# Priority for the closing LayerNorms of a two-layer trunk, and a last column half made in two ranges

## The chip, the cores and the metric

The kernel runs on one core of one Trainium2 chip. The metric is the device time of one launch in microseconds. The kernel before takes 645.32 us, the median of three runs (645.12 to 645.33).

## The reference

A post-norm decoder trunk of two layers on x of 256 tokens by 1024 columns. A conditioning vector c gives six vectors per layer (shift, scale and gate, twice). Each layer is an attention and an MLP, both modulated before and closed with a LayerNorm after. With one block of 256 tokens, the block-sparse attention of layer 0 selects nothing and is plain causal attention.

```python
mod = jnp.einsum('bd,lde->lbe', jax.nn.silu(c), ada_w) + ada_b[:, None, :]
for i in range(DEPTH):                                   # 2 layers
    shift1, scale1, gate1, shift2, scale2, gate2 = [m[:, None, :] for m in jnp.split(mod[i], 6, axis=-1)]
    h = x * (1.0 + scale1) + shift1
    y = moba_attention(h, ...) if i % 2 == 0 else diff_attention(h, ...)
    x = layer_norm(DEEPNORM_ALPHA * x + (1.0 + gate1) * y, ln_g[i, 0], ln_b[i, 0])
    h = x * (1.0 + scale2) + shift2
    y = jnp.square(jax.nn.relu(h @ w_up[i])) @ w_down[i]   # 1024 -> 4096 -> 1024
    x = layer_norm(DEEPNORM_ALPHA * x + (1.0 + gate2) * y, ln_g[i, 1], ln_b[i, 1])
return x
```

## The kernel before

The 256 tokens are two blocks, b = 0 and b = 1, of 128 rows each. All weights stream from HBM once. Every dense product is exact to float32 by three matmuls (`mm3`, L164 to L166, and `dense2`, L181): the operand and the weight are each split into a rounded part and a rest, and hi by hi, hi by lo and lo by hi are added in PSUM. So each weight piece of 128x1024 costs a cast on ScalarE (ACT, L127) and a subtraction on VectorE (DVE, L128), and the activations cost the same.

The order of the work is written by hand in `PROGRAM` as short steps: V and Q make values, queries and keys; S, P, F are attention; O is the output projection; U is the MLP's product upward for one block and 512 of the 4096 columns (24 matmuls), X and Y its squared ReLU and the upward products of both blocks together; D is the product downward; B makes the vectors that a close needs; C closes a sub-layer for one block; E is the end of the last D, for b = 1, by column halves. f takes steps from a queue `filler`: each step is a DMA of 512 KB (L212) and a reduction on DVE (L213) towards the conditioning vectors. Around the first close the program reads `... O01 C00 O10 O11 C10 U00 U01 X00 ...` (for C, the first digit is b and the second says attention or MLP).

A scheduler sets each engine's own order from this: it takes instructions as their inputs become ready in its model, and in a `with tc.high_priority()` block those traced inside go ahead of others that wait. The order is then fixed; every engine runs its own list and waits on semaphores.

A close (`close`, L585) is for one block:

- `layer_norm`: z = accumulator * gate for both halves (DVE, L286), z += alpha * x (L289), statistics (L299, L300), the reciprocal square root on GpSimd (POOL, L274 and L275), the first half normalised on DVE (L305), a bias on DVE (L307), the second half normalised on ACT (L308).
- `modulate`: for each half four transposes on TensorE (PE, L317) into PSUM tile `tp`, scale and shift on ACT (L321), the rounded part hT on ACT (L324) and its rest on DVE (L325). hT is the operand of the next dense products: L164 and L165 use its rounded part, L166 its rest.
- the residual for the next close (L328, L329), which goes to the front of `filler`.

There are eight closes: for each of the two layers, after the attention and after the MLP, b = 0 and then b = 1. The text calls the pairs close 1 (layer 0 attention, at 135 to 159 us), close 2 (layer 0 MLP, 318 to 345), close 3 (layer 1 attention, 440 to 465) and the tail (layer 1 MLP, from 621). In the tail nothing follows: no `modulate`, but the normalised rows go out by DMA in two halves (L591, L594, L596).

The E step for b = 1 does j = 6 and 7 for columns 0 to 511 and then for columns 512 to 1023, 24 matmuls of 128x512 each. Both column halves of b = 1 are two PSUM tiles of tag `sc`, 512 columns each.

Of the kernel before, what the change touches and what calls it, by code (L numbers as in the profile page):

```python
# [36 lines left out]
NJ = FF // 512  # L37
# [29 lines left out]
SHIFT1, SCALE1, GATE1, SHIFT2, SCALE2, GATE2 = range(6)  # L67
C_ID, C_ONE, C_MASK, C_ROPE = 0, 128, 256, 512
C_W = 576


@with_exitstack
def tile_trunk(ctx: ExitStack, tc: tile.TileContext, x, c, moba_w_in, moba_w_out, diff_w_in, diff_w_out,
# [11 lines left out]
    def psum(tag):  # L85
        return psp.tile([P, 512], F32, tag=tag, name=tag, bufs=NB[tag])


    cs = cpool.tile([P, C_W], F32, name="cs")
    ident, ones = cs[:, C_ID:C_ID + P], cs[:, C_ONE:C_ONE + P]  # L90
# [60 lines left out]
    def load_rows(w, r0):  # L151

        ops = []
        for r in range(2):
            raw = raw_tile()
            sp.dma_start(out=raw.rearrange("p (k n) -> p k n", n=1024),
                         in_=w[r0 + r * 256:r0 + (r + 1) * 256, :].rearrange("(k p) n -> p k n", p=P))
            for q in range(2):
                ops.append(split_piece(raw[:, q * 1024:(q + 1) * 1024]))
        return ops  # L160

    def mm3(dst, lhs, rhs, start, stop):
        (xh, xl), (wh, wl) = lhs, rhs
        pe.matmul(dst, lhsT=xh, rhs=wh, start=start, stop=False)  # L164
        pe.matmul(dst, lhsT=xh, rhs=wl, start=False, stop=False)  # L165
        pe.matmul(dst, lhsT=xl, rhs=wh, start=False, stop=stop)  # L166
# [88 lines left out]
    def halves(t, b):  # L255

        return t[:, :, b * P:(b + 1) * P], t[:, :, (2 + b) * P:(3 + b) * P]
# [7 lines left out]
    def split_ops(pair, b):  # L265
        return as_ops([tuple(t[:, :, b * P:(b + 1) * P] for t in pair)])
# [6 lines left out]
    def rsqrt_eps(dst, src):  # L273
        pool_e.tensor_scalar(out=dst, in0=src, scalar1=EPS, scalar2=None, op0=ALU.add)  # L274
        pool_e.tensor_tensor(out=dst, in0=dst, in1=nhalf.to_broadcast(list(src.shape)), op=ALU.pow)  # L275

    def layer_norm(b, accs, gate, parts=None):

        z = ap_.tile([P, D], F32, tag="x", name="z", bufs=3)
        mv = ap_.tile([P, 2], F32, tag="bna", name="bna", bufs=2)  # L280
        rs = ap_.tile([P, 1], F32, tag="rs", name="rs", bufs=2)
        hs = [slice(h * 512, (h + 1) * 512) for h in range(2)]
        for cs_ in ([hs] if parts is None else [[slice(*p)] for p in parts]):
            for c_ in cs_:
                a0 = c_.start % 512
                vec.tensor_tensor(out=z[:, c_], in0=accs[c_.start // 512][:, a0:a0 + c_.stop - c_.start],  # L286
                                  in1=gate[:, c_], op=ALU.mult)
            for c_ in cs_:
                vec.scalar_tensor_tensor(out=z[:, c_], in0=xt[b][:, c_], scalar=ALPHA, in1=z[:, c_],  # L289
                                         op0=ALU.mult, op1=ALU.add)  # L290
            if parts is None:
                w = 512
            else:
                w = 256
            if c_.start == 0 or parts is None:
                st = ap_.tile([P, D // w, 6], F32, tag="bns", name="bns", bufs=2)
            for c_ in cs_:
                for q in range(c_.start // w, c_.stop // w):
                    vec.bn_stats(out=st[:, q, :], in_=z[:, q * w:(q + 1) * w])  # L299
        vec.bn_aggr(out=mv, in_=st)  # L300
        rsqrt_eps(rs, mv[:, 1:2])
        if parts is not None:
            return z, mv, rs
        nm = ap_.tile([P, 1], F32, tag="nm", name="nm", bufs=2)
        vec.tensor_scalar(out=z[:, hs[0]], in0=z[:, hs[0]], scalar1=mv[:, 0:1], scalar2=rs,  # L305
                          op0=ALU.subtract, op1=ALU.mult)
        vec.scalar_tensor_tensor(out=nm, in0=mv[:, 0:1], scalar=-1.0, in1=rs, op0=ALU.mult, op1=ALU.mult)  # L307
        act.activation(out=z[:, hs[1]], in_=z[:, hs[1]], func=AF.Identity, scale=rs, bias=nm)  # L308
        return z

    def modulate(b, z, A, B, tiles):
        for h in range(2):
            hi, lo = halves(tiles[h], b)
            ps = psum("tp")
            full = ap_.tile([P, 512], F32, tag="full", name="full", bufs=2)
            for k in range(4):
                pe.transpose(out=ps[:, k * P:(k + 1) * P], in_=z[:, (h * 4 + k) * P:(h * 4 + k + 1) * P], identity=ident)  # L317
            for k in range(4):
                j = h * 4 + k
                ks = slice(k * P, (k + 1) * P)  # L320
                act.activation(out=full[:, ks], in_=ps[:, ks], func=AF.Identity, scale=A[:, j:j + 1],  # L321
                               bias=B[:, j:j + 1])
            f3 = full.rearrange("p (k t) -> p k t", t=P)
            act.copy(out=hi, in_=f3)  # L324
            vec.tensor_tensor(out=lo, in0=f3, in1=hi, op=ALU.subtract)  # L325

    def residual(b, z, gb, bb):
        vec.tensor_tensor(out=z, in0=z, in1=gb, op=ALU.mult)  # L328
        vec.tensor_tensor(out=z, in0=z, in1=bb, op=ALU.add)  # L329
        xt[b] = z  # L330
# [254 lines left out]
    def close(l, i, b, accs, bd, tiles):  # L585
        A, B, gate, gb, bb = bd
        if A is None:
            parts = ((0, 512), (512, 1024))
            z, mv, rs = layer_norm(b, accs, gate, parts)
            for c0, c1 in parts:  # L590
                vec.scalar_tensor_tensor(out=z[:, c0:c1], in0=z[:, c0:c1], scalar=mv[:, 0:1], in1=gb[:, c0:c1],  # L591
                                         op0=ALU.subtract, op1=ALU.mult)
            for c0, c1 in parts:
                vec.scalar_tensor_tensor(out=z[:, c0:c1], in0=z[:, c0:c1], scalar=rs, in1=bb[:, c0:c1],  # L594
                                         op0=ALU.mult, op1=ALU.add)
                sp.dma_start(out=out[0, b * P:(b + 1) * P, c0:c1], in_=z[:, c0:c1])  # L596
            return
        z = layer_norm(b, accs, gate)
        modulate(b, z, A, B, tiles)
        filler.appendleft(lambda: residual(b, z, gb, bb))  # L600

    def run(program, st):
# [4 lines left out]
    def step_load(st, key, loader):  # L607
        if key not in st:
            st[key] = loader()
        return st[key]  # L610
# [30 lines left out]
    def step_close(st, b, i):  # L641
        l = st["l"]
        if b == 0:
            st["x"] = act_tiles() if st["bd"][0] is not None else None
        close(l, i, b, st["oacc" if i == 0 else "dacc", l, b], st["bd"], st["x"])
# [61 lines left out]
    def step_down_last(st):  # L707

        l = st["l"]
        for c0, c1 in ((0, 512), (512, 1024)):  # L710
            for j in (NJ - 2, NJ - 1):
                lhs = split_ops(st["s", j], 1)
                w = step_load(st, ("wd", l, j), lambda: load_rows(w_down[l], j * 512))
                for k in range(4):
                    mm3(st["dacc", l, 1][c0 // 512][:, c0 % 512:c0 % 512 + c1 - c0], lhs[k],
                        tuple(t[:, c0:c1] for t in w[k]), False, j == NJ - 1 and k == 3)

    w_ins, w_outs = (moba_w_in[0], diff_w_in[0]), (moba_w_out[0], diff_w_out[0])
    seq = [(b, g) for g in range(NG) for b in range(2)]
# [6 lines left out]
        "F": lambda st, n: attend_finish(*on_tiles.pop(n)),  # L726
        "B": step_bound, "O": step_out, "C": step_close,
        "U": step_up, "X": step_up_T, "Y": step_up_both, "D": step_down, "E": step_down_last,
        "L": lambda st, l: st.__setitem__("l", l),
    }  # L730
# [9 lines left out]
def _constants():  # L740

    import numpy as np
    cst = np.zeros((P, C_W), np.float32)
    cst[:, C_ID:C_ID + P] = np.eye(P, dtype=np.float32)
# [35 lines left out]
```

## Time and profile before

| what | value |
|---|---|
| median of 3 runs | 645.32 us |
| the profiled execution, its own time | 644.19 us |
| its span (first to last instruction) | 642.0 us |
| PE busy | 615.6 us, 96% of the span |
| DVE busy | 499.8 us, 78% |
| ACT busy | 377.5 us, 59% |
| POOL busy | 21.7 us, 3% |
| chain that ended last | PE 64%, DVE 18%, DMA 9% |

The profiled execution took 2.2 us more than its span, and lies 1.13 us below the median. All places in the text are in microseconds from the start of the span. In the views, a row is a group of instructions of one line: start, time, engine, line, output and inputs, and in brackets how long the engine had stood idle before it and what ended that. Two instructions in a row on an engine overlap by some tenths of a microsecond, so the distance from one start to the next is what a further instruction costs.

### The profile page before, as it was taken

The page shows a single profiled execution, that of the slowest core. Times are in us where ns is not written, and L with a number is a line of the kernel's source. Part 1 is how long each engine was busy: PE and PEld are TensorE (multiplying, and loading weights), DVE is VectorE, ACT ScalarE, POOL GpSimd, SP SyncE. Part 2 cuts the span into 40 slices and gives each one's busy share as a digit, 9 for nine tenths or more (in the row PEclk, how much of TensorE's full clock was granted, in tenths as well). Part 3 has the DMA queues.
Part 4 walks back from the last instruction along what each step waited for, and adds up shares of the span by engine and source line. Part 5 has one row for each costly group of instructions (what it writes and reads, how often), then busy time and mean ns, then how long its engine had stood idle before and what let it go on. Part 6 is the DMA issues. An engine that isn't in the chain of part 4 may idle for free.

```text
span 642.0 us, 8775 instructions
## 1 busy us (share of the span) xinstructions
PE 615.6 (96%) x3140; PEld 503.5 (78%) x3140; DVE 499.8 (78%) x903; ACT 377.5 (59%) x699; POOL 21.7 (3%) x37
## 2 busy tenths in 40 slices
PE   4999999998999999999999999999999999999994
PEld 3767887886888888888877787777788888888883
DVE  4798998879969788888799988987984646565446
ACT  3448666547836546655477666775785556475530
POOL 0000000001000000000000010011100000000002
PEclk9999999999999999999999999999999999999998
DMA  8996988876688999889875966772663764746401
GB/s 295 407 333 263 319 308 280 286 252 230 205 318 314 316 329 321 318 293 321 290 251 166 351 232 235 259 265 84 205 223 107 261 225 151 249 138 208 186 0 66
DMA packets 65941, 158.23 MB, mean 246 GB/s; under 512 B 4041, under 2 KB 21098, under 8 KB 65898
## 3 DMA queue, kind: packets, MB, share of 16 engines
q1 hardware_dynamic: 65898, 157.68, 70.4%
q8 instruction: 24, 0.39, 0.2%
q14 instruction: 19, 0.16, 0.1%
HBM read 156.62 MB, written 1.05 MB: 246 GB/s over the span
## 4 chain that ended last, share of the span: by engine, by line
PE 64%; DVE 18%; DMA 9%; issue 3%; ACT 3%; POOL 2%; SPq 0%; DVEq 0%; POOLq 0%; ACTq 0%
PE ac L181 12%; PE sc L181 10%; DMA aw<-in_ada_w_dram 7%; PE mm L680 7%; PE tp L680 6%; DVE lo L128 5%; PE mm L164 5%; PE mm L166 5%; PE mm L165 5%; DVE aw L213 5%; PE mm L685 3%; PE tp L685 3%; PE sc L411 1%; ACT hi L127 1%; DVE z L289 1%
## 5 line engine op out<-in xcount | busy, mean ns | idle before, releaser
L128 DVE TENSOR_TENSOR lo<-raw,hi 128x1024 fp32r<-128x1024 f32 x196 | 232.0, 1197 | 43.0 <-ACT hi L127 39.3
L127 ACT CAST hi<-raw 128x1024 fp32r<-128x1024 f32 x196 | 201.0, 1035 | 59.5 <-PE sc L181 43.2
L213 DVE CUSTOM_DVE_ANT_0 aw<-aw,sbc,tabT 128x1024 f32<-128x1024 f32 x96 | 121.9, 1280 | 27.4 <-DMA aw<-in_ada_w_dram 27.2
L164 PE MATMUL mm<-hi,hT 128*128 128x512 f32 x224 | 91.6, 410 | 4.9 <-ACT hi L127 2.3
L166 PE MATMUL mm<-hi,hT 128*128 128x512 f32 x224 | 90.2, 403 | 0.0
L165 PE MATMUL mm<-lo,hT 128*128 128x512 f32 x224 | 89.7, 401 | 0.1
L680 PE MATMUL mm<-hT,hi 128*128 128x512 f32 x192 | 60.0, 394 | 0.0
L680 PE MATMUL tp<-hT,hi 128*128 128x512 f32 x192 | 59.7, 392 | 0.0
L164 PEld LDWEIGHTS mm<-hi,hT 128*128 128x128 f32 x224 | 42.3, 189 | 15.8 <-ACT hT L514 2.8
L181 PE MATMUL ac<-hi,sTh 128*128 128x512 f32 x160 | 50.9, 396 | 0.0
L181 PE MATMUL ac<-hi,sTl 128*128 128x512 f32 x160 | 50.8, 394 | 0.0
L181 PE MATMUL ac<-lo,sTh 128*128 128x512 f32 x160 | 50.2, 394 | 0.0
L166 PEld LDWEIGHTS mm<-hi,hT 128*128 128x128 f32 x224 | 42.4, 189 | 9.8 <-DVE hT L325 0.4
L165 PEld LDWEIGHTS mm<-lo,hT 128*128 128x128 f32 x224 | 42.5, 190 | 9.5 <-DVE lo L128 0.3
L181 PE MATMUL sc<-hi,sTh 128*128 128x512 f32 x144 | 45.1, 392 | 0.0
L181 PE MATMUL sc<-hi,sTl 128*128 128x512 f32 x144 | 44.7, 391 | 0.0
L181 PE MATMUL sc<-lo,sTh 128*128 128x512 f32 x144 | 44.5, 390 | 0.0
L685 PEld LDWEIGHTS mm<-hT,lo 128*128 128x128 f32 x192 | 34.4, 188 | 7.2
L685 PEld LDWEIGHTS tp<-hT,lo 128*128 128x128 f32 x192 | 34.4, 188 | 7.1
L690 ACT COPY nat<-mm 128x256 f32<-128x256 f32 x24 | 7.8, 376 | 52.3 <-PE mm L680 52.3
L685 PE MATMUL mm<-hT,lo 128*128 128x256 f32 x192 | 36.1, 280 | 0.0
L685 PE MATMUL tp<-hT,lo 128*128 128x256 f32 x192 | 36.0, 279 | 0.0
(153 smaller groups left out, 906.7 us busy)
## 6 DMA issues: line engine op xcount, KB each, us to landing
aw<-in_ada_w_dram SPq DMA_DIRECT2D x96, 512.0 KB, 5.8
raw<-in_mlp_w_up_dram SPq DMA_DIRECT2D x32, 1024.0 KB, 5.8
raw<-in_mlp_w_down_dram SPq DMA_DIRECT2D x32, 1024.0 KB, 5.6
raw<-in_diff_w_in_dram SPq DMA_DIRECT2D x16, 512.0 KB, 4.6
raw<-in_moba_w_in_dram SPq DMA_DIRECT2D x24, 256.0 KB, 5.2
raw<-in_moba_w_in_dram SPq DMA_DIRECT2D x8, 512.0 KB, 4.8
raw<-in_moba_w_out_dram SPq DMA_DIRECT2D x4, 1024.0 KB, 8.4
raw<-in_diff_w_in_dram SPq DMA_DIRECT2D x4, 1024.0 KB, 6.7
```

What stands on the lines that cost most here:

```text
L127: act.copy(out=hi[:, :n], in_=raw_ap)
L128: vec.tensor_tensor(out=lo[:, :n], in0=raw_ap, in1=hi[:, :n], op=ALU.subtract)
L164: pe.matmul(dst, lhsT=xh, rhs=wh, start=start, stop=False)
L165: pe.matmul(dst, lhsT=xh, rhs=wl, start=False, stop=False)
L166: pe.matmul(dst, lhsT=xl, rhs=wh, start=False, stop=stop)
L181: pe.matmul(dsts[h], lhsT=a, rhs=w[:, h * 512:(h + 1) * 512], start=start and k == 0 and i == 0, stop=stop and k == n - 1 and i == 2)
L213: vec.tensor_tensor_reduce(out=aw, in0=aw, in1=sbc, scale=1.0, scalar=adab_cols(l, v)[:, j:j + 1], op0=ALU.mult, op1=ALU.add, accum_out=dst)
L289: vec.scalar_tensor_tensor(out=z[:, c_], in0=xt[b][:, c_], scalar=ALPHA, in1=z[:, c_], op0=ALU.mult, op1=ALU.add)
L411: pe.matmul(dst[:, kb * P:(kb + 1) * P], lhsT=qk[b, g][rows, i, :], rhs=qk[kb, g][rows, 2 + i, :], start=True, stop=True)
L680: pe.matmul(ps, lhsT=w[k][0][:, c_], rhs=x3[k], start=first, stop=last)
L685: pe.matmul(ps[:, 0:S], lhsT=w[k][1][:, c_], rhs=x3[k][:, 0:S], start=False, stop=False)
L690: act.copy(out=r[:, i * S:(i + 1) * S], in_=ps[:, S:2 * S])
```

## The change

Two edits. First, `layer_norm` and `modulate` of all closes but the last pair are traced with `tc.high_priority()`; the residual stays as it was. Second, the last pair of closes and the E step use `LAST_RANGES`: columns 0 to 511, 512 to 767 and 768 to 1023. The E step's second half is then 48 matmuls of 128x256 in place of 24 of 128x512; accumulation in the second PSUM tile is ended once, by the last of the 48. The last `layer_norm` does L286, L289 and L299 for three ranges; the last operations and the output DMAs stay in two halves.

```diff
+LAST_RANGES = ((0, 512), (512, 768), (768, 1024))
...
     def close(l, i, b, accs, bd, tiles):
         A, B, gate, gb, bb = bd
         if A is None:
-            parts = ((0, 512), (512, 1024))
+            parts = LAST_RANGES
+            outs = ((0, 512), (512, 1024))
             z, mv, rs = layer_norm(b, accs, gate, parts)
-            for c0, c1 in parts:
+            for c0, c1 in outs:
...
-        z = layer_norm(b, accs, gate)
-        modulate(b, z, A, B, tiles)
+        with tc.high_priority():
+            z = layer_norm(b, accs, gate)
+            modulate(b, z, A, B, tiles)
         filler.appendleft(lambda: residual(b, z, gb, bb))
...
-        for c0, c1 in ((0, 512), (512, 1024)):
+        for c0, c1 in LAST_RANGES:
             for j in (NJ - 2, NJ - 1):
...
-                        tuple(t[:, c0:c1] for t in w[k]), False, j == NJ - 1 and k == 3)
+                        tuple(t[:, c0:c1] for t in w[k]), False, c1 % 512 == 0 and j == NJ - 1 and k == 3)
```

The lines of the changed kernel stand 2 to 4 further down: L286 becomes L288, L289 L291, L299 L301, L300 L302, L305 L307, L307 L309, L317 L319, L325 L327, and L164 to L166 become L166 to L168. The first edit moves instructions at the three closes; these are the places the prediction speaks of.

DVE at close 1, from the end of b = 0's normalising to b = 1's. `sc` is b = 1's accumulator, `ac` b = 0's; the two rows of `hT<-full,hT` are the rests of b = 0's operand, first and second half. Before:

```order
L305 TENSOR_SCALAR z<-z,bna,rs 128x512
L307 SCALAR_TENSOR_TENSOR nm<-bna,rs 128x1
L128 TENSOR_TENSOR lo<-raw,hi 128x1024 x2
L286 TENSOR_TENSOR z<-sc,gate 128x512 x2
L325 TENSOR_TENSOR hT<-full,hT 128x4x128
L289 SCALAR_TENSOR_TENSOR z<-x,z 128x512 x2
L325 TENSOR_TENSOR hT<-full,hT 128x4x128
L299 BN_STATS bns<-z 128x6 x2
L128 TENSOR_TENSOR lo<-raw,hi 128x1024
L300 BN_AGGR bna<-bns 128x2
```

And after:

```order
L130 TENSOR_TENSOR lo<-raw,hi 128x1024 x2
L288 TENSOR_TENSOR z<-sc,gate 128x512 x2
L291 SCALAR_TENSOR_TENSOR z<-x,z 128x512 x2
L301 BN_STATS bns<-z 128x6 x2
L327 TENSOR_TENSOR hT<-full,hT 128x4x128
L302 BN_AGGR bna<-bns 128x2
L327 TENSOR_TENSOR hT<-full,hT 128x4x128
L307 TENSOR_SCALAR z<-z,bna,rs 128x512
L309 SCALAR_TENSOR_TENSOR nm<-bna,rs 128x1
L130 TENSOR_TENSOR lo<-raw,hi 128x1024 x4
```

All six operations on b = 1's z now stand ahead of both rests of b = 0's operand. At closes 2 and 3 the same holds for the second rest (the first stands ahead of them in both kernels).

PE at the same place: the transposes of b = 1 (`tp<-cs,z`, in two sets of four). Before, they stand among the matmuls of U00 and U01, the first set behind 29 of them:

```order
L166 MATMUL mm<-hi,hT 128x512
L164 MATMUL mm<-hi,hT 128x512
L165 MATMUL mm<-lo,hT 128x512
L317 MATMUL tp<-cs,z 128x128 x4
L166 MATMUL mm<-hi,hT 128x512
L164 MATMUL mm<-hi,hT 128x512
L165 MATMUL mm<-lo,hT 128x512
L317 MATMUL tp<-cs,z 128x128 x4
L166 MATMUL mm<-hi,hT 128x512
```

After, they stand behind the first five matmuls, and the rest of U00 is behind them (the row ahead of the first five is the output projection's last):

```order
L183 MATMUL sc<-hi,sTl 128x512 x2
L166 MATMUL mm<-hi,hT 128x512
L167 MATMUL mm<-lo,hT 128x512
L166 MATMUL mm<-hi,hT 128x512
L168 MATMUL mm<-hi,hT 128x512
L166 MATMUL mm<-hi,hT 128x512
L319 MATMUL tp<-cs,z 128x128 x8
L167 MATMUL mm<-lo,hT 128x512
L168 MATMUL mm<-hi,hT 128x512
```

The eight transposes have moved some 24 matmuls towards the front, and the first L168, which needs the first rest, stands ahead of them. At close 2 b = 1's transposes move 7 matmuls towards the front, at close 3 13, and at close 3 those of b = 0 some 8.

DVE in the tail, with the semaphores that each row waits for. Before, b = 1 from its second column half:

```order
L286 TENSOR_TENSOR z<-sc,gate 128x512 [waits PE_49]
L289 SCALAR_TENSOR_TENSOR z<-z 128x512 [waits DVE_49]
L299 BN_STATS bns<-z 128x6 [waits DVE_49]
L299 BN_STATS bns<-z 128x6
L300 BN_AGGR bna<-bns 128x2 [waits DVE_49]
```

And after:

```order
L288 TENSOR_TENSOR z<-sc,gate 128x256 [waits PE_49]
L288 TENSOR_TENSOR z<-sc,gate 128x256
L291 SCALAR_TENSOR_TENSOR z<-z 128x256 [waits DVE_49] x2
L301 BN_STATS bns<-z 128x6 [waits DVE_49] x2
L302 BN_AGGR bna<-bns 128x2 [waits DVE_49]
```

Both ranges of 256 columns stand together, and only the first of them waits for PE: it waits for the end of the accumulation in the tile that both share, which is now the last of the 48 matmuls.

More of the change, by code (lines that the diff above doesn't have):

```diff
@@ L587, in close @@
         if A is None:
-            parts = ((0, 512), (512, 1024))
+            parts = LAST_RANGES
+            outs = ((0, 512), (512, 1024))
             z, mv, rs = layer_norm(b, accs, gate, parts)
-            for c0, c1 in parts:
+            for c0, c1 in outs:
                 vec.scalar_tensor_tensor(out=z[:, c0:c1], in0=z[:, c0:c1], scalar=mv[:, 0:1], in1=gb[:, c0:c1],
                                          op0=ALU.subtract, op1=ALU.mult)
-            for c0, c1 in parts:
+            for c0, c1 in outs:
                 vec.scalar_tensor_tensor(out=z[:, c0:c1], in0=z[:, c0:c1], scalar=rs, in1=bb[:, c0:c1],
```

## The prediction

> **What bounds the kernel now.** I read the page's busy shares first, then what PE waits for from 130 us on, then PE's busy time by stretches, and at last the timelines of PE and DVE at each close.
>
> ```profile
> PE 615.6 (96%) x3140; PEld 503.5 (78%) x3140; DVE 499.8 (78%) x903; ACT 377.5 (59%) x699; POOL 21.7 (3%) x37
> ```
>
> ```profile
> PE tp L317 <- DVE nm L307: 2.1, 3, 0.9
> PE mm L164 <- ACT hT L324: 1.1, 1, 1.1
> PE tp L317 <- DVE z L305: 0.8, 3, 0.3
> ```
>
> ```profile
> 147.40:150.80 3.40, 2.28 (x12) 1.38 (x12) 3.40 (x6) 3.37 (x10) 0.00 (x0) 1.00 0.97 323
> 170.00:300.00 130.00, 130.00 (x660) 110.39 (x659) 108.72 (x147) 74.68 (x105) 0.00 (x0) 1.00 0.90 317
> 345.00:440.00 95.00, 93.81 (x512) 73.40 (x512) 83.03 (x228) 64.73 (x175) 8.39 (x16) 1.00 0.72 250
> 475.00:621.00 146.00, 146.00 (x739) 123.94 (x738) 80.06 (x91) 81.19 (x115) 0.00 (x0) 1.00 0.52 182
> 632.30:635.70 3.40, 0.83 (x4) 0.37 (x2) 2.40 (x5) 0.00 (x0) 0.00 (x0) 1.00 0.00 0
> 635.70:642.00 6.30, 0.00 (x0) 0.00 (x0) 2.83 (x4) 0.00 (x0) 1.63 (x2) 0.52 0.22 83
> ```
>
> PE is the bound. In the rows of stretches the length is followed by the busy time of PE, weight loads, DVE, ACT and POOL, then by the granted clock of PE. Between the closes PE has no gap (130.00 of 130 us, 146.00 of 146), so what a close adds to PE's position is carried to the end: nothing later has slack to take it back. The three rows of waits are nearly all that PE loses to closes, 2.1 + 1.1 + 0.8 = 4.0 us. That caps what priority can gain.
>
> **Close 1 before**, two pieces of DVE's rows and then PE's:
>
> ```profile
> 148.50 1.28 DVE L286 TENSOR_TENSOR z<-sc,gate 128x512 f32<-128x512 f32 x2
> 149.69 0.68 DVE L325 TENSOR_TENSOR hT<-full,hT 128x512 fp32r<-128x512 f32 x1
> 150.29 1.29 DVE L289 SCALAR_TENSOR_TENSOR z<-x,z 128x512 f32<-128x512 f32 x2
> 151.50 0.69 DVE L325 TENSOR_TENSOR hT<-full,hT 128x512 fp32r<-128x512 f32 x1
> 152.10 1.28 DVE L299 BATCH_NORM_STATS2 bns<-z 128x6 f32<-128x512 f32 x2
> 153.30 1.21 DVE L128 TENSOR_TENSOR lo<-raw,hi 128x1024 fp32r<-128x1024 f32 x1
> 154.42 0.20 DVE L300 BATCH_NORM_AGGREGATE bna<-bns 128x2 f32<-128x12 f32 x1
> 154.54 1.17 DVE L128 TENSOR_TENSOR lo<-raw,hi 128x1024 fp32r<-128x1024 f32 x1
> 156.48 0.55 DVE L305 TENSOR_SCALAR z<-z,bna,rs 128x512 f32<-128x512 f32 x1 [0.77 <-POOL rs L275]
> ```
>
> ```profile
> 137.10 1.28 DVE L213 CUSTOM_DVE_ANT_0 aw<-aw,sbc,tabT 128x1024 f32<-128x1024 f32 x1 [1.05 <-DMA aw<-in_ada_w_dram]
> ```
>
> ```profile
> 150.43 0.50 PE L166 MATMUL mm<-hi,hT 128*128 128x512 f32 x1
> ...
> 157.09 0.66 PE L317 MATMUL tp<-cs,z 128*128 128x128 f32 x4 [0.32 <-DVE z L305]
> ...
> 158.05 0.39 PE L165 MATMUL mm<-lo,hT 128*128 128x512 f32 x1
> 158.28 0.60 PE L317 MATMUL tp<-cs,z 128*128 128x128 f32 x4
> 158.64 0.48 PE L166 MATMUL mm<-hi,hT 128*128 128x512 f32 x1
> ```
>
> The reader should see four distances. Two operations on b = 1's z take 1.20 us (148.50 to 149.69). The first rest L325 starts between them, and L166 follows it by 0.74 (149.69 to 150.43). From the statistics' end at L300 to L305 it is 2.06, through POOL. From L305 to the transposes it is 0.61. While DVE and POOL do all this, PE runs U00 and U01, and so the whole detour costs it 0.32.
>
> **Close 1 after.** b = 0's operations on z stand ahead of the reduction that waited 1.05 us for its DMA at 137.10, so that wait is covered, and DVE comes to b = 1's L286 at 148.50 - 1.05 = 147.45. Six operations follow, 3 x 1.20 = 3.6, and the first rest starts at 151.05: 1.36 later than before, though what it reads is there earlier. L166 starts at 151.05 + 0.74 = 151.8. PE is there long before: its output projection loses the 0.87 wait of before, and with three matmuls of U00 (0.23 each, 158.05 to 158.28) it stands at that L166 at about 148.6 to 148.9. It waits 3 us. Behind L166 stands one matmul and then the transposes of b = 1. Their chain: L300 0.60 after the first rest, 151.65; L305 at 153.7; transposes at 154.3. PE waits another 2 us, with all of U00's other 19 matmuls queued behind it. The second set waits for ACT's half of z: before, the two sets stand 1.19 apart with three matmuls (0.7) between; I take 1.0, so 155.3, and 0.37 for the set. U00 goes on at 155.7. The two kernels have issued the same matmuls when the one that started at 158.64 comes up; after, 27 are still ahead of it, 27 x 0.2335 = 6.3, so it starts at 162.0. **Term: +3.35 us.** Ends: 2.5, if each of the four links is 0.2 shorter; 4.0, if ACT is one more operation of 0.6 late.
>
> **Closes 2 and 3**, DVE's and PE's rows:
>
> ```profile
> 338.13 0.20 DVE L300 BATCH_NORM_AGGREGATE bna<-bns 128x2 f32<-128x12 f32 x1
> 340.80 0.66 PE L317 MATMUL tp<-cs,z 128*128 128x128 f32 x4 [0.25 <-DVE z L305]
> ...
> 453.38 1.28 DVE L286 TENSOR_TENSOR z<-sc,gate 128x512 f32<-128x512 f32 x2
> 461.37 0.66 PE L317 MATMUL tp<-cs,z 128*128 128x128 f32 x4 [0.26 <-DVE z L305]
> ```
>
> At close 2 a weight piece (L128, 1.13) now stands behind L300, so L300 starts at 337.0 and the transposes at 337.0 + 2.06 + 0.61 = 339.7. They stand 7 matmuls (1.64) earlier on PE, at a slot of 339.0 - so they wait 0.7 where they waited 0.25. The L166 that needs the second rest waits 0.25 more, as that rest starts 2.4 later, behind four operations. Term +0.65 (0.3 to 1.0). At close 3 L286 comes 0.6 earlier (452.75), the second rest starts 3.6 behind it at 456.35 (before 1.2 behind it), L166 at 457.1 against a slot of 456.2: a wait of 0.85. L300 at 456.95 gives transposes at 459.6, 13 matmuls (3.0) ahead of 461.11, so at a slot of 458.1 + 0.85: 0.65 more of waiting, less the old 0.26. For b = 0, normalising comes 1.9 earlier and the transposes 8 or 9 matmuls (2.0) earlier: +0.15. Term **+1.4** (0.7 to 1.8). b = 0's waits at closes 1 and 2 are within these: the 0.87 and 1.1 of close 1 go, and reappear inside its larger ones.
>
> **The tail.**
>
> ```profile
> 633.17 0.69 DVE L286 TENSOR_TENSOR z<-sc,gate 128x512 f32<-128x512 f32 x1 [1.18 <-PE sc L166]
> 633.90 0.69 DVE L289 SCALAR_TENSOR_TENSOR z<-z 128x512 f32<-128x512 f32 x1
> 634.62 0.75 DVE L299 BATCH_NORM_STATS2 bns<-z 128x6 f32<-128x256 f32 x2
> 635.41 0.26 DVE L300 BATCH_NORM_AGGREGATE bna<-bns 128x2 f32<-128x24 f32 x1
> ```
>
> ```profile
> 511.52 0.64 PE L685 MATMUL mm<-hT,lo 128*128 128x256 f32 x4
> 511.99 0.62 PE L680 MATMUL mm<-hT,hi 128*128 128x512 f32 x2
> ```
>
> The range 512 to 767 could overlap with the matmuls of the last range only if it waited for its own 24; it waits for all 48. From the last matmul to L300 DVE has the same columns in six operations of 256 instead of four (the statistics were 256 wide already): six steps of 0.33, taken from the pair's 0.75 (an operation of 0.42 and a step), and 0.13 to drain, 2.1, against 635.41 - 633.17 = 2.24 with their waits on one another. That is -0.13. Four matmuls of 256 take 0.47 (511.52 to 511.99), 0.1175 each: 48 are 5.64 against 24 x 0.2275 = 5.46, +0.18. b = 0's extra DVE time (four small operations, 0.4) lies in the idle 1.18. Term +0.05; ends -0.15, and +0.5 if in a long run each 256-wide matmul takes 0.01 more.
>
> In the attention of layer 1 (95 us, PE idle 1.19) many rows move by a place or two; I take nothing, with 1 us to either side.
>
> Sum without the clock: 3.35 + 0.65 + 1.4 + 0.05 = +5.45.
>
> **The clock.** In the stretches above, PE was busy for 0.83 of the 3.4 us before 635.7, and from there the clock granted is about half (0.52 as a mean). In close 1 before, the 3.4 us with most waiting still have 2.28 busy, and the clock stays at 1.00. After the change PE does one to two matmuls between 148.9 and 154.3, so any 3.4 us placed in there have 0.6 to 1.0 busy: like the stretch that lost the clock, not like the one that kept it. The price of half clock:
>
> ```profile
> 16.92 0.63 PE L166 MATMUL ac<-hi,hT 128*128 128x512 f32 x1
> 17.34 0.63 PE L165 MATMUL mm<-lo,hT 128*128 128x512 f32 x1
> ```
>
> A matmul then takes 0.42 to 0.43 in place of 0.2335, so 3.4 us at half clock lose 1.5. A fall at 154.3 runs partly over the wait for ACT (1.0 lost), two such stretches lose 2.8. I take 1.5. A rule by which to judge it is in the Trainium skill, "TensorE: Matmul & The Clock Gate", Part 1: The HAM clock gate: a free-running window of about 3.4 us, half clock after one idle window, full clock after a busy one. It does not say how idle "idle" is; the trace puts the limit between 0.83 and 2.28 busy us here. By the rule taken strictly, with no matmul at all in the window, the clock would hold and the sum stay at 5.45.
>
> **The sum.** +5.45 + 1.5 = +6.95. The profiled execution would go from 644.19 to 651.1; it lies 1.13 below the median, and on the median, 645.32, that is 652.3.
>
> **Rivals.**
> - The clock holds: 645.32 + 5.45 = 650.8. For it: PE is never without a matmul for more than 3 us. Against it: the 0.83 row.
> - Faster: priority pays because b = 1's early chain is covered. Its place is DVE at close 1: if b = 0's rests were ready before PE asked for them, PE would lose neither 0.87 + 1.1 nor 0.32 there, and the three closes would give back up to the 4.0 of the waits: 641.3 to 644. It decides at one point: the first rest must start at or before 148.1 (PE's 148.9 less 0.74), and three pairs of 1.20 stand ahead of it from 147.45 on. For it: b = 0's transposes do stand nine matmuls earlier. Against it: DVE's order.
> - No change that can be told (within 0.2%, 1.3 us, about what a measurement of this kernel can tell): b = 1's L286 reaches DVE some 3 us earlier than I count, so that only closes 2 and 3 lose: 644.0 to 646.6. It would need b = 1's output projection to end by 144.5, which PE's order does not allow.
> - The tail's ranges do overlap, as the change says: the first range of 256 goes under the last 24 matmuls, three steps of 0.33 saved, -1.0 on any case. The one wait for PE in DVE's order speaks against it.
>
> **How the numbers follow.** Clock falls 0.47; clock holds 0.36; faster 0.09; no change 0.08. Slower is the first two, 0.83. The likeliest gives 652.3. The range leaves out the last two cases, at the lower end; the clock-holding case with its low ends (2.5 + 0.3 + 0.7 - 0.15 and 1 for attention, some of it) reaches down to about 648; the likeliest with 2.8 for the clock and 4.0 for close 1 reaches 654.3, with the upper ends of closes 2 and 3 655.
>
> **What would show it.** Right: in the 12 us from 146, PE waits about 3 us at an L166 (L168 in the changed kernel) for DVE's rest and about 2 at the transposes for L307, DVE's pairs of b = 1 stand ahead of the first rest, and PE's matmul of 158.64 starts near 162; a clock below 1.00 in the stretch after 154; waits of 0.5 to 0.9 at 457 and 459; in the tail, the 256-wide L288 both start after the last matmul. Wrong: a first rest that starts before 149, or later stretches (170 to 300) in which PE has gaps that shrink, or a clock that stays at 1.00, which takes off 1.5.

## The result, and the profile after

The changed kernel takes 654.11 us (median of four runs, 652.29 to 656.70) against 645.22 us in the same comparison: a ratio of 1.0143 (95% interval 1.012 to 1.0166), 8.9 us slower. Its profiled execution, the shortest of the four, took 652.29 us with a span of 650.2 us, so the two profiled spans differ by 8.2. The comparison of the traces below is of these two executions; where runs scatter, that is said. The ratios leave out one execution, of e10 below, which took 1022.57 us at a mean granted clock of 0.56.

The page's row of engines, and what PE waits for from 130 us on, as shown of before:

```profile
PE 618.1 (95%) x3164; PEld 505.7 (78%) x3164; DVE 500.6 (77%) x907; ACT 377.1 (58%) x699; POOL 22.4 (3%) x37
```

```profile
PE mm L168 <- DVE hT L327: 3.7, 2, 3.1
PE tp L319 <- DVE z L307: 1.6, 3, 0.8
PE tp L319 <- DVE nm L309: 1.1, 2, 0.7
PE mm L452 <- ACT pT L398: 0.9, 1, 0.9
PE tp L471 <- DVE sums L434: 0.7, 1, 0.7
PE tp L396 <- DVE sums L434: 0.6, 1, 0.6
```

The first row is new: L168 (L166 before) waits for DVE's rest, once for 3.1 us. The last three are waits in the attention of layer 1.

Close 1, DVE and then PE:

```profile
147.74 1.28 DVE L288 TENSOR_TENSOR z<-sc,gate 128x512 f32<-128x512 f32 x2
148.94 1.28 DVE L291 SCALAR_TENSOR_TENSOR z<-x,z 128x512 f32<-128x512 f32 x2
150.14 1.28 DVE L301 BATCH_NORM_STATS2 bns<-z 128x6 f32<-128x512 f32 x2
151.33 0.67 DVE L327 TENSOR_TENSOR hT<-full,hT 128x512 fp32r<-128x512 f32 x1
151.93 0.20 DVE L302 BATCH_NORM_AGGREGATE bna<-bns 128x2 f32<-128x12 f32 x1
152.04 0.64 DVE L327 TENSOR_TENSOR hT<-full,hT 128x512 fp32r<-128x512 f32 x1
153.46 0.55 DVE L307 TENSOR_SCALAR z<-z,bna,rs 128x512 f32<-128x512 f32 x1 [0.78 <-POOL rs L277]
```

```profile
148.00 0.50 PE L166 MATMUL mm<-hi,hT 128*128 128x512 f32 x1 [0.26 <-ACT hT L326]
148.34 0.39 PE L167 MATMUL mm<-lo,hT 128*128 128x512 f32 x1
148.56 0.40 PE L166 MATMUL mm<-hi,hT 128*128 128x512 f32 x1
152.06 0.80 PE L168 MATMUL mm<-hi,hT 128*128 128x512 f32 x1 [3.10 <-DVE hT L327]
152.65 0.63 PE L166 MATMUL mm<-hi,hT 128*128 128x512 f32 x1
154.06 1.12 PE L319 MATMUL tp<-cs,z 128*128 128x128 f32 x4 [0.78 <-DVE z L307]
155.41 1.12 PE L319 MATMUL tp<-cs,z 128*128 128x128 f32 x4 [0.23 <-ACT z L310]
156.18 0.78 PE L167 MATMUL mm<-lo,hT 128*128 128x512 f32 x1
```

The three pairs of operations on b = 1's z run, and only then the first rest, at 151.33. PE's third product of U00 has stood since 148.96 for it. The four transposes that took 0.60 to 0.66 us in a row before take 1.12, and a matmul behind a wait or a set of transposes 0.80 or 0.78 where before had 0.50 and 0.48: the clock is halved.

One link got shorter. From the statistics' end to b = 1's normalising it was 2.06 before (L300 at 154.42, L305 at 156.48) and is 1.53 now (151.93 to 153.46). POOL's first operation of that link, before and then after:

```profile
154.71 1.08 POOL L274 TENSOR_SCALAR rs<-bna 128x1 f32<-128x1 f32 x1 [9.05 <-DVE bna L300]
...
152.21 0.55 POOL L276 TENSOR_SCALAR rs<-bna 128x1 f32<-128x1 f32 x1 [9.73 <-DVE bna L302]
```

Both times it ends 0.08 us behind the operation that DVE runs beside it: a weight piece of 1.17 from 154.54 before, the second rest of 0.64 from 152.04 after. So what DVE does right behind the statistics lengthens this link; why is not shown.

The windows show the clock (length, busy time of PE, PEld, DVE, ACT and POOL, clock):

```profile
147.17:150.58 3.41, 1.53 (x6) 0.61 (x4) 3.41 (x6) 2.45 (x6) 0.00 (x0) 1.00 0.91 291
150.58:154.00 3.42, 1.22 (x2) 0.50 (x2) 2.65 (x8) 1.36 (x2) 1.12 (x2) 0.50 0.85 313
154.00:157.41 3.41, 3.12 (x11) 2.53 (x12) 3.41 (x6) 3.41 (x8) 0.00 (x0) 0.50 0.05 19
157.41:160.82 3.41, 3.41 (x16) 2.74 (x16) 3.41 (x5) 1.86 (x5) 0.00 (x0) 1.00 0.99 326
174.00:304.00 130.00, 130.00 (x659) 110.32 (x659) 106.42 (x142) 75.10 (x105) 0.00 (x0) 1.00 0.88 308
350.00:447.00 97.00, 93.34 (x513) 72.95 (x511) 82.45 (x229) 64.00 (x172) 9.63 (x16) 1.00 0.70 238
483.00:629.00 146.00, 146.00 (x739) 123.94 (x738) 80.03 (x91) 81.10 (x115) 0.00 (x0) 1.00 0.53 182
```

Between the closes PE is again without a gap (130.00 of 130, 146.00 of 146), so no lost time is taken back there. The attention of layer 1 has 3.66 us without work in 97, where before had 1.19 in 95. The tail:

```profile
641.48 0.75 DVE L288 TENSOR_TENSOR z<-sc,gate 128x256 f32<-128x256 f32 x2 [1.11 <-PE sc L168]
642.15 0.75 DVE L291 SCALAR_TENSOR_TENSOR z<-z 128x256 f32<-128x256 f32 x2
642.82 0.74 DVE L301 BATCH_NORM_STATS2 bns<-z 128x6 f32<-128x256 f32 x2
643.60 0.26 DVE L302 BATCH_NORM_AGGREGATE bna<-bns 128x2 f32<-128x24 f32 x1
```

Both ranges start together, after the last matmul (641.165): no overlap.

Where the 8.2 us arise can be counted, since PE issues the same number of instructions up to each place. The table is the start of the n-th PE instruction after, less that of before, read near 135, 300, 345, 440 and 475 us of before; each row is what one stretch added, in us. The other columns are experiments told below, one trace each.

| stretch | after | e2 priority alone | e4 priority b = 1 | e6 priority close 1 | e5 priority close 3 | e10 close 1, b = 0 |
|---|---|---|---|---|---|---|
| start to 135 us | +0.3 | -0.1 | +0.9 | -0.1 | 0.0 | -0.1 |
| close 1 | +4.1 | +5.2 | +2.3 | +4.4 | -1.1 | -1.5 |
| close 2 | +0.6 | +0.7 | +1.2 | +1.5 | +2.9 | 0.0 |
| attention of layer 1 | +2.2 | +1.6 | +1.9 | +0.7 | 0.0 | +0.9 |
| close 3 | +0.7 | +0.8 | +0.7 | +0.7 | +0.6 | 0.0 |

In the tail of the changed kernel the last matmul comes another 0.4 later, and from it to the end of the span 0.2 less pass than before. Up to 135 us the order is the same in all these kernels, so the first row shows what executions differ by anyway. At close 1 e5 too has the order of before, and at close 2 PE has it in e5, e6 and e10 (their -1.1, +2.9 and +1.5 are told below). At close 2 and in the attention, the changed kernel, e2, e4 and e7 have one and the same order on every engine.

### The profile page after: what moved, and what is told of

Read it like the earlier page. It is cut to its first block, busy times and chain, and to the rows that moved or that the text cites. A ratio compares the mean times of both kernels' runs of the same rounds, so it can differ in the third digit from the quotient of the medians.

```text
span 650.2 us, 8836 instructions
## 1 busy us (share of the span) xinstructions
PE 618.1 (95%) x3164; PEld 505.7 (78%) x3164; DVE 500.6 (77%) x907; ACT 377.1 (58%) x699; POOL 22.4 (3%) x37
## 3 DMA queue, kind: packets, MB, share of 16 engines
HBM read 156.62 MB, written 1.05 MB: 242 GB/s over the span
## 4 chain that ended last, share of the span: by engine, by line
PE 68%; DVE 14%; DMA 7%; ACT 4%; issue 3%; POOL 2%; SPq 0%; DVEq 0%; POOLq 0%; ACTq 0%
PE ac L183 14%; PE sc L183 10%; PE mm L684 7%; PE tp L684 6%; PE mm L168 5%; PE mm L167 5%; PE mm L166 4%; DVE lo L130 4%; DVE aw L215 3%; PE mm L689 3%; PE tp L689 3%; DMA aw<-in_ada_w_dram 3%; PE sc L413 2%; ACT hi L129 2%; PE tp L396 1%
## 5 line engine op out<-in xcount | busy, mean ns | idle before, releaser
L166 PE MATMUL mm<-hi,hT 128*128 128x512 f32 x224 | 91.3, 408 | 4.1 <-ACT hi L129 2.3
L168 PE MATMUL mm<-hi,hT 128*128 128x512 f32 x224 | 90.7, 405 | 3.8 <-DVE hT L327 3.7
L166 PEld LDWEIGHTS mm<-hi,hT 128*128 128x128 f32 x224 | 42.6, 190 | 15.5 <-ACT hi L129 3.0
L168 PEld LDWEIGHTS mm<-hi,hT 128*128 128x128 f32 x224 | 42.5, 190 | 14.5 <-DVE hT L327 5.2
```

## The experiments

**One edit at a time.** e1 is the changed kernel without the `with tc.high_priority():`, e2 the kernel before with it.

> The second edit alone: LAST_RANGES in the E step and in the last pair of closes, no priority anywhere; the order up to the last 48 matmuls is that of before. Theory (the loss comes from the priority, and the ranges give no overlap, since the one wait for TensorE is for the last of the 48 matmuls): within 0.1% of before, +0.0 to +0.5 us; the last matmul starts 0.2 to 0.4 later than before, and the first 256-wide L288 (or L286) of b = 1 after the last matmul. Rival (the ranges overlap): 0.7 to 1.0 us faster than before, and a 256-wide multiplication that starts before the last matmul. Rival (the ranges are part of the loss): 1 us or more slower.

> The first edit alone: high priority in all closes but the last pair, the tail as before. Theory: 7.5 to 9 us slower than before, nearly all of the change's loss; the same waits on TensorE as in the changed kernel (about 3.1 us at the third rounded product of U00 for DVE's rest, 0.8 at the transposes), and again a clock of 0.5 for 3.4 or 6.8 us from about 151. Rival (the two edits only lose together): less than 3 us slower.

Measured: the ranges alone 1.0013 (0.9990 to 1.0037), median 644.32 us beside 644.79; priority alone 1.0134 (1.0121 to 1.0147), 652.73 us. So the whole loss that can be told is the priority's, and the ranges give no gain. In e1's trace the last matmul lies 0.42 us further from PE's 2947th instruction (at 593.49 before) than before, and from its start to the aggregation 2.44 us pass, not 2.66. That is +0.42 - 0.22 = +0.2.

**Which block loses.** The condition `if b == 0` (or `b == 1`) decides whether the close has priority.

```diff
-        z = layer_norm(b, accs, gate)
-        modulate(b, z, A, B, tiles)
+        with (tc.high_priority() if b == 0 else __import__("contextlib").nullcontext()):
+            z = layer_norm(b, accs, gate)
+            modulate(b, z, A, B, tiles)
```

> Priority for the closes of b = 0 alone; b = 1's closes and the tail as before. In DVE's order both rests of b = 0's operand then stay ahead of b = 1's z operations but for one. Theory (b = 0's priority pays, b = 1's is what loses): close 1 gains about 1.5 us (the waits of 0.87 and 1.12 go, one of 0.1 to 0.3 comes), close 3 0.3; 643.4 us, 0.9965 to 0.9980 of before, and the clock stays at 1.00 up to the end. Rival (any priority loses, since it puts transposes where TensorE has to wait): 1 us or more slower. Rival (nothing left to gain, later waits take it back): within 0.1%.

> Priority for the closes of b = 1 alone. Theory: DVE runs six z operations of b = 1 ahead of the first rest of b = 0, so the rest starts at 152.1, TensorE waits 2.6 us at U00's third rounded product and 1.6 at b = 1's transposes, and close 1 costs 3.2 us and up to 1.5 for the clock; closes 2 and 3 0.6 and 1.0; with what the attention of layer 1 lost in the changed kernel (2.2) 6 to 8.5 us slower than before. Rival (the loss comes from b = 0's transposes standing earlier): less than 2 us slower.

Measured: b = 0 alone 0.9996 (0.9975 to 1.0018), no difference that can be told; b = 1 alone 1.0099 (1.0081 to 1.0117), 6.2 us slower in the medians. b = 1's priority is what loses, by DVE's order. In e4 the six operations on b = 1's z stand ahead of the first rest again, and PE waits for it:

```profile
152.55 0.50 PE L166 MATMUL mm<-hi,hT 128*128 128x512 f32 x1 [2.30 <-DVE hT L325]
```

Close 1 cost 2.3 there, less than the 3.2 and more that were expected: b = 1's transposes stand behind eight matmuls of U00 and not five, and did not wait. In e3 the first rest stands between b = 1's two multiplications:

```profile
148.13 0.68 DVE L286 TENSOR_TENSOR z<-sc,gate 128x512 f32<-128x512 f32 x1
148.73 0.68 DVE L325 TENSOR_TENSOR hT<-full,hT 128x512 fp32r<-128x512 f32 x1
149.33 0.68 DVE L286 TENSOR_TENSOR z<-sc,gate 128x512 f32<-128x512 f32 x1
```

and PE does not wait for it. In e3's trace PE gained 1.54 us at close 1, as expected, but lost 0.4 at close 2, 0.4 in the attention and 0.2 at close 3. The expected 1.8 us are not in the times.

**Which close.** Two kernels with priority for both blocks at one close alone (conditions `(l, i) == (1, 0)` and `(l, i) == (0, 0)`).

> Priority at close 3 alone (layer 1 after the attention, both b); everything up to there, the attention of layer 1 too, in the order of before. Theory (each close has its own price, and the attention loses only where its own order was changed): the position of TensorE moves by 0.5 to 1.0 us at close 3 and not before it; 0.5 to 1.0 us slower. Rival (the attention's 1.6 to 2.2 us come from the priority at close 3, which follows it): 2 us or more slower, with the waits of 0.9 and 0.5 at the attention's end.

> Priority at close 1 alone (layer 0 after the attention, both b). The orders of closes 2 and 3 are those of before, but the scheduler's later choices in the attention of layer 1 change too. Theory: close 1 costs 3.35 us and 0.7 to 1.8 for the clock, 4.1 to 5.2 together, close 2 nothing, and the attention of layer 1 loses 0.5 to 2.2 through its changed order: 5 to 7.4 us slower. Rival (the attention's loss needs the orders of closes 2 and 3): 4.1 to 5.2 us slower, with no waits in the attention beyond those of before.

Measured: close 3 alone 1.0029 (1.0005 to 1.0052); close 1 alone 1.0088 (1.0056 to 1.0121). e5's median is 2.1 us above before's, more than the 0.5 to 1.0 that were expected, but its interval reaches from 0.3 to 3.3 us and its trace speaks against the rival: the attention, which keeps its order, loses nothing (1.82 us behind before at its start and at its end), and close 3 loses 0.6. The rest of that trace's loss lies at close 2, whose order is that of before. In e6 priority at close 1, 200 us earlier, changes the scheduler's choices in the attention, and it loses 0.7; close 3, whose order changed as well (the expectation had that wrong), loses 0.7. One trace does not size such a loss. In the other traces with the attention in the order of before, the stretch added 0.3 (e9), 0.4 (e3), 0.7 (e11), 0.9 (e10) and 1.2 (e1). So e6's 0.7, with a third order, is no more than executions of one order differ by. The four traces with the changed kernel's order there, 1.6 (e2), 1.9 (e4), 2.2 (e7) and 2.2, lie above all six, and all four show two waits of PE that the six do not: 0.4 to 1.3 at L450 for the copy of the probabilities, and 0.7 at L469 for their sums. So the order that the attention gets as a by-product costs about 1.4 us by the means of the two groups (2.0 and 0.6). Which row of it costs what was not tried one by one.

**The clock.** e7 keeps all the priority and fills the wait with matmuls whose sums are overwritten.

```diff
+        if (st["l"], b, j) == (0, 0, 0):
+            for _ in range(12):
+                pe.matmul(ps, lhsT=block_ops(st["x"], b)[0][0], rhs=w[0][0], start=True, stop=True)
         dense(ps, block_ops(st["x"], b), w)
```

> All closes with priority, tail as before, and U00's first rounded product of layer 0 is issued 12 times more ahead of it (each is overwritten; 12 x 0.2335 = 2.8 us of TensorE work inside its wait of 3.1). The scheduler then puts b = 1's transposes behind 8 matmuls of U00 and not 5, and the second set behind two more. Theory (the clock falls because TensorE stands idle for most of a 3.4 us window): the rest is waited for only some 0.3 us, the clock stays at 1.00 at close 1, and the matmul that started at 158.64 in before starts 2.2 us later (155.7 + 22 x 0.2335 = 160.85), not 4.1 to 5.2: 4.5 to 6.5 us slower than before in all. Rival (the clock falls there for another reason): 0.5 again for 3.4 us or more at 150 to 156, and 3.2 us or more at close 1. Rival (the added matmuls delay the close): 4 us or more at close 1 with the clock at 1.00.

Measured: 1.0077 (1.0044 to 1.0109), 649.7 us beside 652.73 of e2, which has no such matmuls (from two sets of runs). The mean granted clock of e7's executions is 0.995 to 0.997 but for one, that of e2's 0.988 to 0.992. Windows and PE's two waits of e7:

```profile
148.16:151.57 3.41, 3.20 (x14) 2.26 (x12) 3.41 (x7) 1.23 (x4) 0.00 (x0) 1.00 1.01 362
151.57:154.98 3.41, 2.76 (x14) 1.90 (x15) 2.63 (x7) 3.05 (x5) 1.12 (x2) 1.00 0.39 155
...
151.66 0.50 PE L166 MATMUL mm<-hi,hT 128*128 128x512 f32 x1 [0.30 <-DVE hT L325]
153.66 0.66 PE L317 MATMUL tp<-cs,z 128*128 128x128 f32 x4 [0.57 <-DVE z L305]
```

The clock stays at 1.00, and close 1 costs 1.6 us in place of 4.1 to 5.2, with twelve matmuls more to do. (Close 2 adds 1.0, the attention 2.2 and close 3 0.7, about what they add in the other kernels, and so e7 is still 5.6 us slower than before.) Part of the saving is the clock, part the transposes' later place (behind eight matmuls, not five). What the clock alone cost in the changed kernel can be added up from its rows. Up to the second set of transposes at 155.41 PE waited for DVE and ACT, and the half clock cost nothing. From there the set took 0.77 in place of 0.37, and three matmuls 0.57, 0.43 and 0.34 (starts at 156.18, 156.75, 157.18 and 157.52) in place of 0.32, 0.23 and 0.23: 1.0 us, an estimate from these rows. It leaves about 3.2 of close 1's 4.1 for the order. e2 shows how the price varies: its order at close 1 is that of the changed kernel, but its windows lie otherwise.

```profile
149.61:153.02 3.41, 0.73 (x2) 0.30 (x2) 2.70 (x6) 1.68 (x2) 1.09 (x2) 1.00 0.98 338
153.03:156.44 3.41, 2.75 (x11) 2.30 (x12) 3.36 (x5) 2.72 (x7) 0.02 (x1) 0.50 0.10 41
156.44:159.85 3.41, 3.41 (x10) 2.64 (x9) 3.41 (x4) 2.43 (x6) 0.00 (x0) 0.50 0.80 253
```

Here a whole window of full work, 156.44 to 159.85, runs at half clock (10 matmuls, where the changed kernel's window from 157.41 has 16), and close 1 costs 5.2, not 4.1.

**Where the gain of b = 0's priority goes.** The wait for an aw row at 318 us was my first suspect.

> The kernel before with a third buffer for the rows of the conditioning matrix (aw; to make room, p has 6 buffers in place of 8), no priority, no ranges. The scheduler's order moves in many places, the attention of layer 0 among them. It asks whether the wait of DVE for the DMA of aw at 318 us (3.9 before, 4.1 with priority for b = 0, 5.6 in the run with the ranges alone) is what takes back at close 2 what close 1 gains: the third reduction of a row waits for a DMA that could start only when the first had read its buffer. Theory: that wait shrinks to under 2 us and TensorE's 0.59 at close 2 goes; 0 to 2 us faster, if the attention of layer 0 with fewer p buffers loses nothing. Rival (the DMA queue itself is late there): the wait stays at 3 us or more, and the time within 0.2% or slower.

> Priority at close 1 for b = 0 alone, all else as before. Theory: close 1 gains 1.5 us, as it did with priority for b = 0 at all closes; 0.4 of it is taken back at close 2, where DVE waits for the DMA of an aw row whose time does not depend on TensorE, and up to 0.4 in the attention of layer 1, whose order is that of before; close 3 loses nothing. 0.5 to 1.5 us faster (0.9977 to 0.9992). Rival (the gain is given back in full, as in the run with priority for b = 0 at all closes): within 0.1%.

e8 was 1.0133 times as long (1.0090 to 1.0175): the reordered attention of layer 0 lost 6 us before 116 us, with a clock of 0.5 from 109.87. For the question it is a partial answer. DVE's longest wait for aw around close 2 is 2.5 us, not under 2, and PE's position is 5.5 us behind before ahead of close 2 and 5.6 behind it, so the hoped-for 0.59 did not come; but there too the order is another.

e10 gave 1.0005 (0.9980 to 1.0031), median 644.9 beside 644.14: no gain that can be told, and the expectation missed. In its trace PE is 1.5 us ahead of before after close 1, and close 2, with a wait for aw of 3.9 as before, takes back nothing, so my suspect was wrong for this trace. Two other things show. 0.9 goes at the end of the attention, where DVE stands before an aw row that hasn't landed, with L479 behind it for which PE waits (DVE first, then PE's wait in that stretch):

```profile
430.31 1.28 DVE L213 CUSTOM_DVE_ANT_0 aw<-aw,sbc,tabT 128x1024 f32<-128x1024 f32 x1 [0.81 <-DMA aw<-in_ada_w_dram]
...
PE tp L394 <- DVE sTl L479: 0.8, 1, 0.8
```

And most of the 1.5 was never there to win. e5 has the order of before up to close 3, and in its trace the row that DVE waited 1.05 us for at 137.10 had landed:

```profile
135.99 1.28 DVE L213 CUSTOM_DVE_ANT_0 aw<-aw,sbc,tabT 128x1024 f32<-128x1024 f32 x1
```

There PE does not wait at b = 0's transposes at all, and is 1.1 us ahead of before's profiled execution after close 1, with no change made. In e1's trace, the same order again, DVE waits 0.41 and PE is 0.65 ahead. So the wait of 1.05, on which both my walk and the 1.5 rest, is that execution's. Against e5's the priority of b = 0 (e3's 1.54) gains 0.4, against e1's 0.9.

**The tail with a tile of its own.** In e9 the E step adds columns 768 to 1023 into a fresh PSUM tile; DVE finishes columns 512 to 767, and all older sums, beforehand, and adds the last range at the end.

```diff
+                    own = c0 == 768
+                    if own and j == NJ - 2 and k == 0:
+                        st["tail"] = psum("mm")
...
+                        vec.tensor_tensor(out=t_, in0=tail[:, 0:256], in1=gate[:, 768:1024], op=ALU.mult)
+                        vec.tensor_tensor(out=z[:, 768:1024], in0=z[:, 768:1024], in1=t_, op=ALU.add)
```

> No priority; the tail's ranges with a PSUM tile of their own for the last one: the E step adds columns 768 to 1023 of j = 6 and 7 into a fresh tile, so that the tile with columns 512 to 767 (and the older sums of 768 to 1023) is complete 24 matmuls before the end. b = 1's L286 and L289 then run on that tile as 512 columns under the last 24 matmuls, and behind the last matmul stand one multiplication of 256 columns, one addition of 256 and one L299, three small operations where the change has six. Theory (the ranges gave nothing because the shared tile is waited for as a whole): the aggregation starts 1.2 to 1.5 us after the last matmul's end, not 2.2, and the kernel is 0.5 to 0.9 us faster than before (0.9986 to 0.9992). Rival (nothing overlaps even so, or the 48 narrow matmuls take it back): within 0.1% or slower.

> Both of the last two edits together: priority for b = 0 at close 1 and the last range in a tile of its own. Theory: the gains add, since one is at 145 us and the other behind the last matmul: 1.0 to 2.4 us faster than before (0.9963 to 0.9985). Rival (the wait for DMA at 318 us sets the time of what follows in most executions): no more than the tail's part, 0.5 to 0.9.

Measured: e9 1.0015 (0.9989 to 1.0042), e11 0.9995 (0.9970 to 1.0019), median 643.47 beside 644.14. Neither can be told from no change by its time. The traces settle the mechanism. The tail of e11:

```profile
632.52 0.43 DVE L307 BATCH_NORM_STATS2 bns<-z 128x6 f32<-128x256 f32 x1
632.87 0.41 DVE L305 TENSOR_TENSOR on<-mm,gate 128x256 f32<-128x256 f32 x1
633.31 0.43 DVE L306 TENSOR_TENSOR z<-z,on 128x256 f32<-128x256 f32 x1
633.77 0.43 DVE L307 BATCH_NORM_STATS2 bns<-z 128x6 f32<-128x256 f32 x1
634.23 0.26 DVE L308 BATCH_NORM_AGGREGATE bna<-bns 128x2 f32<-128x24 f32 x1
```

DVE works without a gap through the end of the matmuls (the last starts at 632.22), and the aggregation starts 2.01 us after that start, where before needed 2.66 and the ranges of the change 2.44. From the last matmul's end it is 1.73, where 1.2 to 1.5 were expected. So the overlap is there once the tiles are apart; but of the 0.65 the 48 narrow matmuls take back 0.42, and 0.2 are left, where 0.5 to 0.9 were expected. No version here is shown to beat the kernel before.

## Why the prediction was right, point by point

The forecast, 652.3 us and slower, agrees in direction, and 654.11 lies in the range. The mechanism at the closes was the one forecast, but that the total came so near is in part luck: the attention lost 2.2 us that I had put at nothing, and closes 1 and 3 together 1.4 less than I had. By its terms, on the two profiled executions:

- **Close 1, walk: 3.35.** Right against the execution it was made from, with errors in it that offset each other. Forecast and measured: first rest 151.05 and 151.33, L166 151.8 and 152.06, aggregation 151.65 and 151.93, L305 153.7 and 153.46, transposes 154.3 and 154.06, the second set 155.3 and 155.41, U00 on at 155.7 and 156.18. The first three are late by the 0.3 of this execution's later start. The link through POOL was 1.53 and not 2.06, which I had taken over from an order with a weight piece behind the statistics. The two sets came 1.35 apart and not 1.0, and the second took 0.77 and not 0.37, at half clock. Of the wait of 2 us at the transposes only 0.78 shows as a wait, since the two matmuls ahead took 1.22 at half clock where I had 0.47. The matmul of 158.64 started at 163.12, where I had 162.0 without the clock. What it took for a property of the kernel before, the aw row late by 1.05, was one execution's (e5 above): against an execution with that row in time the same order costs 1.1 more.
- **Close 1, clock: 1.5, with 1.0 to 2.8 as ends.** The clock did fall, in every trace with both blocks' priority at close 1 and no filling matmuls (after, e2, e6), and in e4's. Walk and clock together were 4.85; measured 4.1, 5.2 and 4.4. In the changed kernel it fell earlier than I said, at 150.58 and not at 154.3, after a window with 1.53 busy and not 0.6 to 1.0, so most of it lay over waits, and it cost about 1.0 (the estimate above).
- **Close 2: +0.65.** Measured 0.6 (after), 0.7 (e2), 1.0 (e7) and 1.2 (e4), the four traces with this order; DVE's longest wait for an aw row there was 4.0, 4.1, 4.0 and 4.6.
- **Close 3: +1.4.** Over-sized: 0.6 to 0.8. For b = 0 I added 0.15; its wait fell from 0.70 to 0.37 instead, and b = 1's two waits came to 0.64 and 0.41, where I had 0.85 and 0.65.
- **The attention of layer 1: nothing, 1 us to either side.** This is the step that failed: 1.6 to 2.2 us. I counted the moved rows as noise, since before's PE idles only 1.19 us there. A stretch with little slack to gain has much to lose from an order that was not chosen for it. The four traces with this order against the six with that of before show the order to be the cause, and e6 that a priority 200 us earlier suffices to change an order.
- **Tail: +0.05.** Measured +0.2: DVE's chain gained 0.12 (2.24 to 2.12), as forecast; from the last matmul's start to DVE's it is another 0.11 less, which I had not counted; and the 48 narrow matmuls cost 0.42, not 0.18: (5.46 + 0.42) / 48 = 0.1225 each, not 0.1175 as in a run of four. No overlap, as forecast.

Of the rivals, the one of a clock that holds was the nearer alternative; by the estimate above it was worth about 1.0 us in the changed kernel's trace, and e2, with the same order and other windows, paid 1.1 more. The rival of a gain failed at the point it named: the first rest started at 151.33, not by 148.1. Only without b = 1's priority does that point turn (e3, e10), and there the gain was too small to measure.

## What to carry to other kernels

Priority for a critical chain is also precedence over whatever stands beside it, and here the second block's statistics took precedence over the first block's last operand, for which the bound engine was already waiting. Give priority to what the bound engine needs next (all of one block's close, rests included, before the other block's), and read the two orders side by side for the first instruction that moved behind something longer than it. Here priority for b = 0 alone came nearest to that: it cost nothing, but gained nothing that could be told either. And where a list scheduler sets the order, look at the stretches one did not touch: their order changes too.

## What the runs showed that I had not expected

The clock is decided in windows on a fixed grid. In every trace the times between its changes, but for the last, which the end of the trace cuts off, are multiples of 3.413 us (6.827 and 136.533 in e2, 133.12 in the changed kernel, 314.03 in e1). At the closes, PE busy for 1.53 us of such a window at full clock, or for 1.12 or less, was followed by half clock; for 1.81 (e6), 2.08 (e4) or 2.29 (before, from 147.86) it was not. At half clock a window with 2.75 busy was not enough to restore it, one with 3.12 was. The row of e6 that held, and e1's that did not:

```profile
332.05:335.46 3.41, 1.81 (x12) 1.65 (x13) 2.64 (x5) 1.80 (x5) 0.79 (x2) 1.00 0.59 194
...
326.42:329.83 3.41, 1.12 (x8) 1.02 (x8) 2.65 (x5) 1.29 (x4) 1.50 (x2) 1.00 0.75 256
329.83:333.24 3.41, 3.41 (x11) 2.81 (x10) 3.41 (x4) 3.33 (x10) 0.00 (x0) 0.50 0.87 281
```

These are no limits for other work. In e9's trace PE was busy for 2.60 us of a window in the attention of layer 0, where the order is that of before, and half clock followed; it stayed through the next window, in which PE was busy all the time:

```profile
75.06:78.47 3.41, 2.60 (x24) 2.41 (x24) 3.41 (x6) 2.30 (x8) 0.00 (x0) 1.00 0.98 328
78.48:81.89 3.41, 3.41 (x16) 2.76 (x16) 3.14 (x7) 1.69 (x4) 0.00 (x0) 0.50 0.88 305
```

The first window held only narrow matmuls (operands of 64x128 and 128x64, where the closes have 128x512) and two waits of 0.64 and 0.25; before, PE has no gap there and keeps its clock. So the time that PE is busy does not by itself decide; what does was not tried.

e1's close 2 has the order of before. There DVE waited 5.6 us for an aw row in place of 3.9, and a window fell under the limit; that execution lost 2.8 us at close 2 and took 647.45 us, eight of the other eleven of the same kernel 643.6 to 644.7. So a late DMA can cost a window of half clock as well. e5's trace shows the same (2.9 at close 2, an aw row waited for 5.8 us, clock 0.5 from 329.46), and e9's, 4.2 us behind before from 82 us on, the fall in the attention. Such windows go with the larger scatter between executions: of the 68 of before that were measured beside the experiments, the 7 above 647 us have mean granted clocks of 0.991 to 0.994, and the other 61 have 0.995 to 0.997. What started the fall in those was not traced. In e6 the row was waited for 5.3 us, PE lost 1.5 at close 2, and the window with 1.81 busy kept its clock.

The Trainium skill, "TensorE: Matmul & The Clock Gate", Part 1: The HAM clock gate, gives the window of about 3.4 us and the half clock, and the traces agree (3.413 us, a granted clock of 0.50). It lets the clock fall after an idle window; the traces show it fall after windows that were busy for 45% at a close (1.53 of 3.41) and for 76% in e9.
